# The gates of a two-layer encoder as one ScalarE Silu in place of Tanh, a scaled copy and a VectorE product

## The chip, the cores and the metric

The kernel runs on one core of one Trainium2 chip. The metric is the device time of one execution in microseconds (us), the median of the runs shown. A core has a matrix engine (TensorE; PE in the profile, PEld its weight loads), VectorE (DVE), ScalarE (ACT), GpSimd (POOL) and SyncE (SP); SP's and POOL's queues issue the DMA transfers here.

## What is computed

Two layers over 256 tokens of width 4096, in float32. Each layer normalises its input, projects it through one matrix of 4096 by 11264 into eight parts, runs 16 heads of attention (4 key and value heads) and 8 heads of a retention in both directions, gates both results by a silu of two of the projected parts, and projects the gated result back by a matrix of 4096 by 4096. Cut to what matters here:

```python
h = rmsnorm(x, norm_w[l])
proj = h @ w_in[l]
aq, ak, av, ag, rq, rk, rv, rg = jnp.split(proj, SPLIT_POINTS, axis=-1)
...
a_out = (jax.nn.silu(ag) * gqa_attention(aq, ak, av)).astype(x.dtype)
...
r_out = (jax.nn.silu(rg.astype(jnp.float32)) * r).astype(x.dtype)
x = x + jnp.concatenate([a_out, r_out], axis=-1) @ w_out[l]
```

The row's normalisation factor (`rstd`) is applied after the projection: the kernel multiplies the unnormalised input with the weights, and each consumer scales its part of the product by `rstd`, one number for each token.

## The kernel before

**Matrix products.** Each float32 operand is split into a high part, which TensorE takes in one pass, and a low part, the remainder; a product is three matmuls: high by high and low by high (line 1461), high by low (line 1471). The weights are the 512-wide side. They arrive from memory in raw tiles (`wraw`), are cast by ScalarE into the high part (`whi`), and VectorE subtracts to make the low part (`wlo`). Some row pairs use a scheme of seven products in place of eight, for which VectorE makes sums of the weights (`wsum`) first. High and low parts live in a ring of `RING` = 5 pages. A few pages are "far": GpSimd's queue makes their low part with an adding DMA (`fhi`, `flo`).

**Stages.** The work is 11 column blocks of the input projection and 4 of the output projection, for each of two layers. When a block is done, its result stands in two tiles `ca` and `cb` (tokens on the partitions, two row halves of 512 columns), and a task takes it: a gate is always `ca` of the blocks `ag` (four a layer, with the queries) and `rg` (four a layer, with the values). There are thus 16 gates in the program.

**Who follows a gate.** In `attention_group` the gated tile is transposed by VectorE (`turned`) and stored by four DMAs of POOL's queue to `g_dram`, to be fetched later and multiplied with the attention's result. In `retention_pair` the gate comes after the retention weights are there; then `values` makes the high and low part of the values (`vh` by ScalarE, `vl` by VectorE), then two times `retention_head` runs its products on TensorE and multiplies its result into the gate's tile.

**Order.** Every engine's order is written out in advance by a planner in the kernel's Python. `Clock` wraps VectorE and ScalarE: each recorded instruction adds an estimated cost to the engine's `until`, and `now.t` follows TensorE through 0.2268 us for each 512-wide matmul. Between matmuls `tick` asks `room` whether enough weight pages are ready ahead, and if so lets one of the waiting tasks do a step (up to a `yield`). After a step that ends in `yield "PE"` the task's matmuls are put `PE_REST` = 1.8 us behind its last planned instruction. The planner's costs:

```python
def vector_cost(name, n, kwargs):
    one = name in ("tensor_copy", "tensor_scalar", "tensor_scalar_mul", "tensor_scalar_add", "memset")
    return V_FIXED + n * (0.00052 if one else 0.00104)

def scalar_cost(name, n, kwargs):
    return S_FIXED + n * 0.00083 + (0.2 if kwargs.get("accum_out") is not None else 0.0)
```

with `V_FIXED` 0.07 and `S_FIXED` 0.16, and n the elements of a row. All VectorE and ScalarE instructions carry line 248, the line of the recorder, in the profile; they are told apart by their tiles. Working tiles come from 13 pages; a task starts only if the number of pages it pledges (`NEED`: 3 for `ag`, 4 for `rg`) is free.

**Other ScalarE functions.** Exp is used in the attention (`pr`, 64 instructions in 32 pairs) and for the retention's decay matrices (`D`, 8 instructions), and at the start; elsewhere there are copies, casts, squares and one Abs. Tanh occurs in the gates alone.

Of the kernel before, what the change touches and what calls it, by code (L numbers as in the profile page):

```python
# [13 lines left out]
AF = mybir.ActivationFunctionType  # L14
ALU = mybir.AluOpType
AX = mybir.AxisListType

P = 128
# [9 lines left out]
NB = 512  # L28
# [3 lines left out]
MT = SEQ // P  # L32
# [187 lines left out]
class Now:  # L220


    t = 0.0
# [39 lines left out]
def hybrid_encoder(  # L263
# [16 lines left out]
    ve, ac = Clock(nc.vector, vector_cost, now), Clock(nc.scalar, scalar_cost, now)  # L280
# [4 lines left out]
    sp = ctx.enter_context(tc.tile_pool(name="sp", bufs=1))  # L285
# [10 lines left out]
    def t(pool, shape, tag, bufs=None, dt=F32):  # L296
        kw = {} if bufs is None else {"bufs": bufs}
        return pool.tile(shape, dt, tag=tag, name=tag, **kw)
# [7 lines left out]
    def own(n):  # L306

        if current[0]:
            current[0].own += n

    def drop(n=1):

        held[0] -= n
        own(-n)

    def page(shape, name, dt=F32):

        held[0] += 1
        own(1)
        assert held[0] <= PAGES, name  # L320
        return sp.tile(shape, dt, tag="pg", name=name, bufs=PAGES)
# [69 lines left out]
    def rsqrt(dst, ss, n, count):  # L391

        ve.tensor_scalar(dst, ss, 1.0 / count, EPS, op0=ALU.mult, op1=ALU.add)
        nc.gpsimd.tensor_tensor(dst, dst, half[:, :n], op=ALU.pow)
# [617 lines left out]
    def gate(acc, L):  # L1012

        e = page([P, MT, NB], "tanh")
        for m in range(MT):
            h = L.hrstd[:, m : m + 1]
            ac.activation(e[:, m, :], acc[:, m, :], AF.Tanh, scale=h)  # L1020
            ac.activation(acc[:, m, :], acc[:, m, :], AF.Copy, scale=h)
        yield
        ve.scalar_tensor_tensor(acc, e, 1.0, acc, op0=ALU.add, op1=ALU.mult)
        drop()
        yield

    def attention_pair(g, h, kv, qT, rs, done):
# [69 lines left out]
    def attention_group(L, g, gacc, qacc):  # L1097
        def gates():
            yield from gate(gacc, L)
            room = page([P, KG * SEQ], "room")  # L1100
            turned(gacc, room)
            drop()
            yield 0.0
            store(room, g_dram[g % 2])

        yield from gates()
        while "aq" not in L.tables:
            yield
        rs = yield from rotary(qacc, L, "aq", q_dram[g % 2])
        yield STORE  # L1110
        L.rs[g] = rs
# [117 lines left out]
    def retention_pair(L, i, gacc, vacc):  # L1229
        while i not in L.weights:  # L1230
            yield
        wT = L.weights.pop(i)
        yield from gate(gacc, L)
        v = yield from values(vacc, L)
        yield
        for e in range(2):
            yield from retention_head(wT, v, gacc, e)
        users.discard(("h", L.index, i))
        own(2)
        drop(4)  # L1240
        pledge(2)
        room = page([P, KG * SEQ], "room")
        turned(gacc, room)
        if 4 + i < NCH - 2:
            drop()
            yield 0.0
            store(room, next_dram[4 + i])
            put(4 + i, None, 2 * L.index + 1)
        else:
            yield  # L1250
            mixT = gacc.rearrange("p m n -> p (m n)")
            yield from move(room, mixT)
            drop()
            put(4 + i, mixT, 2 * L.index + 1)
# [38 lines left out]
    def rstd_of(L, parts, n):  # L1293

        L.rstd = t(sp, [P, MT], "rstd", 2)
        L.hrstd = t(sp, [P, MT], "hrstd", 2)
        ve.tensor_reduce(L.rstd, parts, axis=AX.X, op=ALU.add)
        rsqrt(L.rstd, L.rstd, MT, D_MODEL)
        ve.tensor_scalar_mul(L.hrstd, L.rstd, 0.5)

    def in_task(L, kind, i, c):
        while L.rstd is None:
# [221 lines left out]
    def out_task(l, n, res):  # L1524
# [19 lines left out]
        if n == N_OUT - 1:  # L1544
            rstd_of(layers[l + 1], sums[:, :, :N_OUT], N_OUT)
# [111 lines left out]
    def first_sums():  # L1657
        load_small()
        part = t(sp, [P, MT, N_OUT], "sums", 2)
        loaded = []  # L1660
        for n in range(N_OUT + 2):
            if n < N_OUT:
                loaded.append(page([P, MT, NB], "x"))
                nc.sync.dma_start(loaded[-1], rows(x[:, columns(n)]))
            yield LANDING / 2
            if n >= 2:
                v = loaded.pop(0)
                for m in range(MT):
                    ac.activation(v[:, m, :], v[:, m, :], AF.Square, accum_out=part[:, m, n - 2 : n - 1])
                drop()  # L1670
        rstd_of(layers[0], part[:, :, :N_OUT], N_OUT)
        whole = page([P, 2 * SEQ], "dist")
        nc.sync.dma_start(whole, consts[:, C_D:C_END])
        yield LANDING / 2
        ac.copy(dist, whole)
        drop()
        log_sigmoid()
        yield
# [154 lines left out]
```

## Time and profile before

| what | value |
|---|---|
| median of 3 runs | 2624.57 us (2623.66 to 2625.17) |
| the profiled execution's own time | 2624.09 us |
| its span, first to last instruction | 2622.3 us |
| granted TensorE clock, mean | 0.998 |
| TensorE busy | 2604.2 us, 99% |
| VectorE busy | 2231.7 us, 85% |
| ScalarE busy | 1684.6 us, 64% |

The span is what the profile shows; the execution's own time is 1.8 us longer. The rows that the prediction quotes come from the profile's page, from groups of instructions (count, busy time, mean duration, idle time just before them and who ended it), from waits (who waited for whom: total, times, longest), from tables of stretches of the span, and from the timeline (start, duration, engine, line, operation, tiles, and in brackets the idle time before it).

### The profile page before, as it was taken

The numbers are of one execution on the slowest core, as the hardware profiler recorded it, in microseconds if no ns is written. First come the engines' busy times: TensorE is split into PE (matmuls) and PEld (weight loads), VectorE is DVE, ScalarE is ACT, GpSimd is POOL, SyncE is SP. The second block draws the span as 40 slices with busy tenths as digits, with TensorE's granted clock in tenths as the row PEclk, the third lists the DMA queues.
The fourth block names the chain that finished last, engine by engine and source line by source line (L and its number), as shares of the span: only waits on it lengthen the run. The fifth ranks groups of instructions, "written<-read, shape, count | busy, mean of one in ns | idle before, by whom it ended". The sixth has DMA issues, their size and how long they took to land.

```text
span 2622.3 us, 33965 instructions
## 1 busy us (share of the span) xinstructions
PE 2604.2 (99%) x11650; PEld 2151.5 (82%) x11650; DVE 2231.7 (85%) x2666; ACT 1684.6 (64%) x2411; POOL 274.6 (10%) x413
## 2 busy tenths in 40 slices
PE   9999999999999999999999999999999999999998
PEld 7888888888888888888888888888888888878886
DVE  8798988898878889777998889898997798897768
ACT  7776667656555778556785666676565566775545
POOL 0010221120001000111101101211100010000000
PEclk9999999999999999999999999999999999999999
DMA  7888887877667766777767777778766666656775
GB/s 287 291 263 261 266 266 240 295 241 235 211 217 235 232 227 214 259 261 255 276 219 230 257 237 265 255 239 276 249 225 209 217 227 217 227 201 220 240 235 188
DMA packets 187151, 633.58 MB, mean 242 GB/s; under 512 B 22624, under 2 KB 29280, under 8 KB 186976
## 3 DMA queue, kind: packets, MB, share of 16 engines
q1 hardware_dynamic: 147760, 521.27, 56.6%
q0 software_dynamic: 39216, 110.12, 15.9%
q8 instruction: 91, 1.49, 0.2%
q14 instruction: 84, 0.69, 0.1%
HBM read 587.27 MB, written 44.04 MB: 241 GB/s over the span
## 4 chain that ended last, share of the span: by engine, by line
PE 94%; DVE 3%; issue 1%; ACT 1%; DMA 1%; SPq 0%; DVEq 0%; POOLq 0%; POOL 0%; ACTq 0%
PE M L1461 60%; PE M L1471 30%; DVE wlo L248 1%; PE M L945 1%; PE M L944 1%; PE M L943 1%; DMA wraw<-in_w_in 1%; DVE wsum L248 1%; PE M L1455 0%; ACT whi L248 0%; ACT ca L248 0%; DMA flo<-in_w_in 0%; DVE ca L248 0%; DVE x7l L248 0%; DVE ls L248 0%
## 5 line engine op out<-in xcount | busy, mean ns | idle before, releaser
L248 ACT CAST whi<-wraw 128x1024 fp32r<-128x1024 f32 (+1 forms) x912 | 878.5, 978 | 529.8 <-PE M L1461 346.2
L248 DVE TENSOR_TENSOR wlo<-wraw,whi 128x1024 fp32r<-128x1024 f32 (+1 forms) x912 | 1007.5, 1127 | 156.3 <-ACT whi L248 147.6
L1461 PE MATMUL M<-whi,x8h 128*128 128x512 f32 x2042 | 795.7, 390 | 0.2 <-DVE cb L248 0.2
L1461 PE MATMUL M<-whi,x8l 128*128 128x512 f32 x2042 | 795.2, 389 | 0.0
L1471 PE MATMUL M<-wlo,x8h 128*128 128x512 f32 x2042 | 586.3, 389 | 0.0
L1461 PE MATMUL M<-whi,x7h 128*128 128x512 f32 x1442 | 561.2, 389 | 1.0 <-ACT whi L248 1.0
L1461 PE MATMUL M<-whi,x7l 128*128 128x512 f32 x1442 | 561.0, 389 | 0.0
L248 ACT CAST whi<-wsum 128x1024 fp32r<-128x1024 f32 x300 | 315.9, 1053 | 212.4 <-PE M L1461 105.2
L1461 PEld LDWEIGHTS M<-whi,x8h 128*128 128x128 f32 x2042 | 383.4, 188 | 80.8 <-DVE cb L248 1.3
L1461 PEld LDWEIGHTS M<-whi,x8l 128*128 128x128 f32 x2042 | 383.4, 188 | 79.0 <-DVE x7l L248 0.2
L1471 PEld LDWEIGHTS M<-wlo,x8h 128*128 128x128 f32 x2042 | 382.1, 188 | 78.8
L1471 PE MATMUL M<-wlo,x7h 128*128 128x512 f32 x1442 | 442.1, 390 | 2.7 <-DVE wlo L248 2.4
L248 DVE TENSOR_TENSOR wlo<-wsum,whi 128x1024 fp32r<-128x1024 f32 x300 | 365.9, 1220 | 42.6 <-ACT whi L248 42.4
L1471 PEld LDWEIGHTS M<-wlo,x7h 128*128 128x128 f32 x1442 | 269.5, 188 | 63.3 <-DVE wlo L248 8.2
L1461 PEld LDWEIGHTS M<-whi,x7h 128*128 128x128 f32 x1442 | 270.7, 188 | 57.8 <-ACT whi L248 1.4
L1461 PEld LDWEIGHTS M<-whi,x7l 128*128 128x128 f32 x1442 | 270.7, 188 | 56.3
L248 DVE TENSOR_TENSOR wsum<-wraw 128x1024 f32<-128x1024 f32 x150 | 182.5, 1216 | 29.9 <-DMA wraw<-in_w_out 14.0
L506 POOL DMA_DIRECT2D flo<-in_w_in x32 | 29.2, 912 | 819.5 <-ACT flo L248 814.4
L248 DVE TENSOR_TENSOR wsum<-wsum,wraw 128x512 f32<-128x512 f32 x150 | 103.8, 692 | 5.2
L248 DVE TENSOR_TENSOR wsum<-wraw,wsum 128x512 f32<-128x512 f32 x150 | 102.4, 683 | 0.1
L248 DVE TENSOR_TENSOR cb<-cb,M 128x512 f32<-128x512 f32 x90 | 60.8, 679 | 23.8 <-PE M L1471 23.8
L248 ACT ACTIVATE pr<-M,st,rs 128x256 f32<-128x256 f32 x64 | 35.5, 559 | 48.5 <-DVE st L248 48.5
(232 smaller groups left out, 1961.3 us busy)
## 6 DMA issues: line engine op xcount, KB each, us to landing
wraw<-in_w_in SPq DMA_DIRECT2D x700, 512.0 KB, 4.5
wraw<-in_w_out SPq DMA_DIRECT2D x256, 512.0 KB, 4.4
flo<-in_w_in POOLq DMA_DIRECT2D x32, 512.0 KB, 7.4
full<-next_dram POOLq DMA_DIRECT2D x18, 512.0 KB, 8.4
kv<-kv_dram POOLq DMA_DIRECT2D x16, 512.0 KB, 7.4
p_dram<-room POOLq DMA_DIRECT2D x64, 128.0 KB, 2.9
pT<-p_dram POOLq DMA_DIRECT2D x16, 512.0 KB, 9.3
flo<-in_w_out POOLq DMA_DIRECT2D x11, 512.0 KB, 7.6
```

Of the source, the lines that this page charges most:

```text
L248: return call(out, *args, **kwargs)
L506: nc.gpsimd.dma_start(g.lo[h], g.src[0][:, h, :], accum_op=ALU.add)
L943: nc.tensor.matmul(out, a[0], b[0], start=start, stop=False)
L944: nc.tensor.matmul(out, a[0], b[1], start=False, stop=False)
L945: nc.tensor.matmul(out, a[1], b[0], start=False, stop=stop)
L1461: nc.tensor.matmul(acc[name], a[i], g.hi[h], start=m == first[name] and not i, stop=False)
L1471: nc.tensor.matmul(acc[name], a, g.lo[h], start=False, stop=m == final[name])
```

## The change

`gate` is Silu with the row's `rstd` as its scale, in place, one instruction for each row half. The Tanh into a page of its own, the copy scaled by half of `rstd`, VectorE's (tanh + 1) times the copy, the page, one `yield`, and the tile `hrstd` go.

```diff
@@ gate
-        e = page([P, MT, NB], "tanh")
         for m in range(MT):
-            h = L.hrstd[:, m : m + 1]
-            ac.activation(e[:, m, :], acc[:, m, :], AF.Tanh, scale=h)
-            ac.activation(acc[:, m, :], acc[:, m, :], AF.Copy, scale=h)
-        yield
-        ve.scalar_tensor_tensor(acc, e, 1.0, acc, op0=ALU.add, op1=ALU.mult)
-        drop()
+            ac.activation(acc[:, m, :], acc[:, m, :], AF.Silu, scale=L.rstd[:, m : m + 1])
         yield
@@ rstd_of
         L.rstd = t(sp, [P, MT], "rstd", 2)
-        L.hrstd = t(sp, [P, MT], "hrstd", 2)
         ve.tensor_reduce(L.rstd, parts, axis=AX.X, op=ALU.add)
         rsqrt(L.rstd, L.rstd, MT, D_MODEL)
-        ve.tensor_scalar_mul(L.hrstd, L.rstd, 0.5)
```

## The prediction

> **What bounds the kernel now.** I read the page's busy line first, then a table of stretches of the span, then TensorE's own waits. In the table the columns are the stretch, its length, and for PE, PEld, DVE, ACT and POOL the busy time with the instruction count in brackets; then the granted clock, the DMA share and GB/s.
>
> ```profile
> PE 2604.2 (99%) x11650; PEld 2151.5 (82%) x11650; DVE 2231.7 (85%) x2666; ACT 1684.6 (64%) x2411; POOL 274.6 (10%) x413
> ...
> 0.00:25.00 25.00, 23.05 (x71) 12.59 (x72) 13.02 (x21) 16.49 (x30) 0.20 (x4) 1.00 0.92 348
> 25.00:590.00 565.00, 564.77 (x2530) 467.60 (x2529) 499.86 (x616) 382.50 (x589) 85.08 (x130) 1.00 0.81 264
> 590.00:600.00 10.00, 9.03 (x40) 6.95 (x39) 8.16 (x10) 6.53 (x10) 0.00 (x0) 1.00 0.63 230
> 600.00:1020.00 420.00, 420.00 (x1920) 350.22 (x1919) 357.64 (x438) 278.22 (x382) 33.75 (x48) 1.00 0.68 223
> 1020.00:1040.00 20.00, 19.67 (x85) 15.63 (x85) 19.90 (x25) 17.42 (x25) 0.90 (x1) 1.00 0.74 236
> 1275.00:1320.00 45.00, 44.58 (x194) 35.59 (x193) 44.39 (x63) 34.07 (x53) 3.58 (x4) 1.00 0.76 239
> 2325.00:2345.00 20.00, 18.42 (x79) 14.34 (x78) 18.95 (x24) 15.01 (x23) 0.00 (x0) 1.00 0.48 168
> 2345.00:2609.00 264.00, 263.68 (x1162) 217.52 (x1161) 206.76 (x225) 141.40 (x175) 9.51 (x11) 1.00 0.67 220
> 2609.00:2622.30 13.30, 1.03 (x5) 0.53 (x3) 4.42 (x10) 2.84 (x6) 0.56 (x1) 0.69 0.84 311
> ```
>
> TensorE is the bound, and nearly without holes. Of the 18.1 us in which it is idle (2622.3 less 2604.2), 1.95 lie in the first 25 us and 12.27 in the tail after the last products. Between, 3.85 us are left: 0.23 before 590, 0.97 around 595, 0.33 around 1030, 0.42 around 1300, 1.58 around 2335 and 0.32 after it. Where it runs, 420 us hold 1920 matmuls, 0.219 us each, at a granted clock of 1.00. Who ends its idle time:
>
> ```profile
> PE M L1471 <- DVE wlo L248: 2.4, 5, 1.3
> PEld M L1471 <- DVE wlo L248: 8.2, 15, 1.7
> ```
>
> The holes are low halves of the weights that VectorE brings late (8.2 us in 15 waits on the weight-load side, parts of which the pipelined matmuls cover). So a change on ScalarE or VectorE moves the time only by making such waits, or by taking some of these few microseconds away. How much the gates' engines have to spare where the gates run is the next table: 12 us around four of the gates, and the sum over such stretches around all 16.
>
> ```profile
> 710.00:722.00 12.00, 12.00 (x56) 10.01 (x55) 10.37 (x12) 8.88 (x11) 0.00 (x0) 1.00 0.37 132
> 882.00:894.00 12.00, 12.00 (x58) 10.05 (x57) 11.04 (x13) 8.87 (x11) 0.00 (x0) 1.00 0.39 137
> 972.00:984.00 12.00, 12.00 (x54) 9.94 (x53) 11.58 (x23) 11.94 (x23) 0.00 (x0) 1.00 0.53 182
> 2270.00:2282.00 12.00, 12.00 (x55) 9.91 (x54) 11.58 (x22) 11.94 (x23) 0.00 (x0) 1.00 0.54 181
> sum 192.00, PE 192.00 PEld 159.20 DVE 177.93 ACT 168.40 POOL 32.76; mean PE 12.00 PEld 9.95 DVE 11.12 ACT 10.52 POOL 2.05
> ```
>
> TensorE is busy 192.00 of 192.00 us: no gate costs it anything today. ScalarE and VectorE are crowded there (168.4 and 177.9), most of all at the last gate of each layer, 972 and 2270.
>
> **What goes.** The groups of the gate (busy us in all, mean ns of one, idle before), and the one table load of the program:
>
> ```profile
> L248 ACT ACTIVATE ca<-ca,hrstd 128x512 f32<-128x512 f32 x32 | 23.2, 726 | 1.0
> L248 ACT ACTIVATE tanh<-ca,hrstd 128x512 f32<-128x512 f32 x32 | 22.9, 715 | 0.2 <-DVE ca L248 0.2
> L248 ACT ACT_TABLE_LOAD x1 | 1.3, 1283 | 0.7 <-PEq L1822 0.7
> ...
> L248 DVE SCALAR_TENSOR_TENSOR ca<-tanh,ca 128x1024 f32<-128x1024 f32 x16 | 19.6, 1225 | 8.8 <-ACT ca L248 8.5
> L248 DVE TENSOR_SCALAR hrstd<-rstd 128x2 f32<-128x2 f32 x2 | 0.3, 170 | 1.7 <-POOL rstd L394 1.7
> ```
>
> Sixteen gates, two row halves each. The 32 scaled copies go: 23.2 us of ScalarE. The 16 products go: 19.6 us of VectorE, with 8.8 us of its waiting for ScalarE just before them. The two `hrstd` multiplications go, 0.3 us and 1.7 us of waiting. The page `tanh` goes, but each gate's task pledges 3 or 4 pages whether it holds them or not, so no other task starts earlier for it. All this is beside a TensorE that is busy 192.00 of 192.00 us: worth nothing by itself.
>
> **What comes.** 32 Silu in the place of 32 Tanh: same shape, same per-row scale operand, so I take the Tanh's 715 ns, and the difference is nothing. What the trace doesn't show is whether Silu lives in the table that is loaded once at the start and serves Exp and Tanh alike. If it does, no load is added. If not, each gate that follows an Exp loads a table and each Exp that follows a gate loads the other: at most 16 and 16, 32 times 1.283 = 41 us of ScalarE. I take the loads as coming, as the dearer end. The Trainium skill, ScalarE: Activation LUTs, section What ACT_TABLE_LOAD costs, gives 2.66 us for a switch, the 1.28 us load and a drain of 1.38 us; by that it would be an estimated 85 us of ScalarE, and the load row above bears out the 1.28, while no row shows the drain, as nothing runs ahead of that load.
>
> Where the loads fall decides. First the way back to Exp:
>
> ```profile
> 0.74 1.28 ACT L248 ACT_TABLE_LOAD   x1 [0.74 <-PEq L1822]
> 2.03 0.22 ACT L248 ACTIVATE lg<-half 128x16 f32<-128x16 f32 x1
> ...
> 0.81 0.07 DVE L248 MEMSET half<- 128x16 f32 x1 [0.81 <-PEq L1822]
> ...
> ACT pr L248 <- DVE st L248: 49.5, 19, 4.4
> ACT D L248 <- DVE D L248: 16.3, 8, 2.7
> ```
>
> The load began at 0.74, before the operand of its Exp was begun (0.81): it doesn't sit behind the Exp's wait. And an Exp that follows a gate usually finds ScalarE idle: all 8 Exps of the decay matrices wait, 2.0 us on average, and those of the attention 19 times, 2.6 us on average. A load of 1.28 us goes into that idle time. So the way back costs nothing in most places; where it isn't hidden, it delays casts by 1.3 us, and for these there is the lead below.
>
> Then the gate itself, here the one at 712:
>
> ```profile
> 710.43 2.00 ACT L248 CAST whi<-wraw 128x1024 fp32r<-128x1024 f32 x2 [4.38 <-PE M L1461]
> 712.33 0.72 ACT L248 ACTIVATE tanh<-ca,hrstd 128x512 f32<-128x512 f32 x1
> 713.72 0.71 ACT L248 ACTIVATE tanh<-ca,hrstd 128x512 f32<-128x512 f32 x1
> 715.09 1.04 ACT L248 CAST whi<-wraw 128x1024 fp32r<-128x1024 f32 x1
> 716.04 1.33 ACT L248 ACTIVATE vh<-cb,rstd 128x512 fp32r<-128x512 f32 x2
> 718.63 1.41 DVE L248 SCALAR_TENSOR_TENSOR vl<-cb,rstd,vh 128x512 fp32r<-128x512 f32 x2
> 721.67 0.28 PE L944 MATMUL M<-vl,wTh 128*128 128x256 f32 x1
> ...
> ACT whi L248 <- PE M L1461: 451.3, 436, 4.4
> ```
>
> The gate now holds ScalarE from 712.33 to 715.09, 2.76 us. After the change it is 1.28 for the load and two Silu at the step from one Tanh to the next halved, (713.72 − 712.33) / 2 = 0.70 each: 2.68 us. ScalarE is done 0.1 us sooner, and VectorE has 1.23 us less to do. With a drain as long as the load (an estimate from the load's row, 1.28) it is 3.96, 1.2 us later. Either is below the lead of the casts: they go round a ring of five pages, 436 of them wait for TensorE to free a place, 451 us in all, and the pair just before this gate waited 4.38 us for that. A cast that waits so has four filled pages ahead of it; four pages of a seven-product pair hold 7 products of 3 matmuls, 7 · 3 · 0.219 = 4.6 us, and those of plain pairs 4 · 4 · 3 · 0.219 = 10.5 us. Nothing becomes late by 1.2 us. Next is the product that the gate's task issues: TensorE reads `vl` at 721.67, `vl` ends at 720.04, 1.63 us earlier, and began 1.26 us after `vh` ended (717.37). So there are 2.9 us between `vh` and the matmul.
>
> Last, the planner. It writes the order of the engines from its own costs, here (0.16 + 512 · 0.00083) = 0.585 us for each gate instruction on ScalarE and 1.13 us for VectorE's. It will see 1.17 us in place of 2.34, and nothing on VectorE, and know of no load; so the steps after a gate move up by 1 to 2 us, in the order of ScalarE, VectorE and TensorE alike. Where they stand then I can't read from this trace. Bounds: below, the late low halves at 1030 and 2335, in stages that the crowded gates 972 and 2270 run into, go away: −(0.33 + 1.58) = −1.9 us. Above, all holes between 25 and 2609 double: +3.85. I take 0, since at all 16 gates the nearest rows show TensorE without any idle time.
>
> **Sum.** ScalarE −23.2 + 41 (none of it ahead of TensorE), VectorE −19.6 (none ahead of TensorE), planner 0: the profiled execution stays at 2624.1 (span 2622.3 and 1.8 around it). The median of the runs shown, 2624.57, is 0.5 above that, so 2624.6. 0.2% is 5.2 us, about what a measurement of this kernel can tell from no change.
>
> **Rivals.**
>
> *Every switch reaches TensorE.* The Trainium skill, ScalarE: Activation LUTs, section Table sets: the hidden batching unit, says to batch calls by table set and not by function, and this change does the opposite, putting Silu between Exps. The mechanism here: the gates' loads, unknown to the planner, use up the lead. That decides if casts at the gates have less than 1.28 us of it. Price: 16 loads of 1.28 = 20.5, so 2645. For it: the ScalarE rows at 972 and 2270, 11.94 of 12. Against: the 4.38 us wait just ahead of the load, and the copies' 1.4 us given back in the same place.
>
> *The values come late.* The planner's view of a gate is off by 2.76 − 2.34 = 0.42 us today; it would be off by 2.68 − 1.17 = 1.51, or 2.79 with the drain, 1.1 to 2.4 us more. `retention_pair` goes from the gate straight to `values` and to products whose place in TensorE's order is planned from there. With VectorE's product gone, `vl` can stand right behind `vh`, and the 1.26 us between them is no longer there; then 2.4 less the remaining 1.63 is a stall of 0.8 us at each of 8 retention gates: +6.2, so 2631. It decides from a lateness of 1.63 us; with the bare load, 1.1, there is none.
>
> *VectorE's relief fills the holes.* The holes are late low halves, and VectorE gets 19.6 us. All of them gone is −3.85: 2620.7. Against: of the holes only those at 1030 and 2335 come within 65 us behind a gate. It isn't even 0.2%.
>
> *No loads at all*, since Silu is in the table of Exp: ScalarE falls by 23 us, the time is the same 2624.6.
>
> **How the numbers follow.** Forecast, with or without loads, within a few microseconds: 0.69. Holes filled: 0.10, half of it counted as over 0.2% for what pipelined matmuls hide of the 8.2 us. Late values or another planned step that comes late, 5 to 8 us: 0.14. Every switch: 0.07. Faster 0.05, same 0.74, slower 0.21. The range goes from the filled holes, 2620.7, to the late values with a little of the doubled holes at the stage ends, 2632; every switch and half of the filled holes are left out.
>
> **What would show it.** Table loads: some 30 of 1.28 us, those before Exp in idle time ended by VectorE; ScalarE about 18 us up, VectorE 20 us down; the windows around the gates still with TensorE at 12.00. Wrong it is if waits of TensorE for `whi`, `wlo` or `vl` appear within 15 us behind a gate, or if the stages at 595, 1030, 1300 and 2335 show several times their idle time.

## The result and the profile after

The change makes the kernel slower by a little: 2630.09 us (2628.11 to 2631.64, 13 runs) against 2623.76 (2623.25 to 2625.6, 13 runs), a ratio of 1.0023 with a 95% interval of 1.0015 to 1.0032. Forecast was 2624.6, with a range from 2620.7 to 2632. The profiled execution took 2629.94 us, its span is 2628.2.

First the page's busy line and the stretches that answer to those of before (columns as there; the time has moved by 1 to 6 us, so the last two are cut a little later), with the stretch from 2190 to 2300 added:

```profile
PE 2606.6 (99%) x11650; PEld 2151.0 (82%) x11650; DVE 2214.9 (84%) x2648; ACT 1697.1 (65%) x2408; POOL 273.8 (10%) x413
...
25.00:590.00 565.00, 563.28 (x2520) 465.66 (x2519) 494.75 (x610) 386.80 (x589) 84.98 (x130) 1.00 0.79 263
590.00:600.00 10.00, 9.41 (x41) 7.32 (x40) 7.25 (x8) 4.78 (x6) 0.00 (x0) 1.00 0.68 250
600.00:1020.00 420.00, 418.78 (x1912) 348.46 (x1911) 355.16 (x438) 283.48 (x390) 34.39 (x48) 1.00 0.68 224
1020.00:1040.00 20.00, 20.00 (x90) 16.56 (x89) 19.34 (x23) 14.96 (x18) 0.89 (x1) 1.00 0.67 207
2190.00:2300.00 110.00, 107.01 (x491) 87.19 (x490) 97.44 (x144) 83.02 (x143) 6.23 (x9) 1.00 0.59 202
2325.00:2345.00 20.00, 20.00 (x90) 16.55 (x89) 18.99 (x21) 12.61 (x14) 0.00 (x0) 1.00 0.55 183
```

VectorE has 16.8 us less to do, as taken out, and ScalarE 12.5 us more. The holes at 1030 and 2335 are gone. New ones stand in 600 to 1020 (1.22 us) and in 2190 to 2300 (2.99 us), where TensorE had none before, and in 25 to 590 (1.72 us, 0.23 before). Who ends them, for TensorE's matmuls and then, for 2190 to 2300 alone, its weight loads:

```profile
PE M L1453 <- DVE cb L248: 3.6, 4, 1.3
PE M L1453 <- ACT whi L248: 2.1, 3, 1.2
PE M L1463 <- DVE wlo L248: 0.8, 4, 0.3
...
PEld M L1463 <- DVE wlo L248: 2.9, 5, 0.7
PEld M L1453 <- ACT whi L248: 2.1, 2, 1.6
PEld M L1453 <- DVE cb L248: 1.4, 1, 1.4
```

Late low halves were known from before. Late `cb`, the adding up of a finished block, is nearly new (one wait of 0.2 us before). Late high halves have grown; before, there was one, the hole around 595, in a row that the prediction doesn't show:

```profile
PE M L1461 <- ACT whi L248: 1.0, 1, 1.0
```

Short holes don't show in the stretches, as the matmuls overlap; laid matmul by matmul against the profile of before, TensorE ends 5.5 us later. The delay grows by 5.3 us between 2190 and 2300 and by 1.9 us between 890 and 1000; 0.9 us is given back at 1030 and 2.2 us at 2335, where the old holes are gone. 1.4 us arise at 95, ahead of the first gate, where both programs are the same (1.3 us of the waits for `cb` above are there). The second profile of the change (below) has 0.5 us there, and a run without loads 0.3, so the rest belongs to that execution and not to the change.

What the table loads do is seen in ScalarE's groups:

```profile
L248 ACT ACT_TABLE_LOAD x30 | 38.5, 1283 | 27.5 <-DVE st L248 22.4 <-DMA pT<-p_dram 4.0 <-PEq L1814 0.7
L248 ACT ACTIVATE ca<-ca,rstd 128x512 f32<-128x512 f32 x44 | 29.4, 716 | 0.8 <-DVE ca L248 0.7
```

29 loads came, 15 ahead of a gate and 14 on the way back, each 1283 ns. The 32 Silu are among the 44 of the second row (12 scaled copies of keys have the same tiles); the mean is 716 ns, that of the Tanh. The number to see is the 27.5 us of idle time just before the loads, 22.4 of them ended by `st`: those loads began when the wait was over. With the 4.0 us ended by `pT`, they are 8 loads, each ahead of an Exp of the attention.

### The profile page after: what moved, and what is told of

Same layout as the page of the kernel before. It is cut to its first block, busy times and chain, and to the rows that moved or that the text cites. A ratio compares the mean times of both kernels' runs of the same rounds, so it can differ in the third digit from the quotient of the medians.

```text
span 2628.2 us, 33961 instructions
## 1 busy us (share of the span) xinstructions
PE 2606.6 (99%) x11650; PEld 2151.0 (82%) x11650; DVE 2214.9 (84%) x2648; ACT 1697.1 (65%) x2408; POOL 273.8 (10%) x413
## 4 chain that ended last, share of the span: by engine, by line
PE 87%; DVE 6%; DMA 3%; issue 2%; ACT 2%; SPq 0%; POOL 0%; DVEq 0%; POOLq 0%; ACTq 0%
PE M L1453 56%; PE M L1463 28%; DVE wlo L248 3%; DMA wraw<-in_w_in 3%; PE M L945 1%; PE M L944 1%; PE M L943 1%; ACT whi L248 1%; DVE wsum L248 1%; DVE x7l L248 0%; ACT ca L248 0%; DVE xf L248 0%; DVE cb L248 0%; DVE x8l L248 0%; DMA full<-in_xT 0%
## 5 line engine op out<-in xcount | busy, mean ns | idle before, releaser
L248 ACT CAST fhi<-wraw 128x1024 fp32r<-128x1024 f32 (+1 forms) x44 | 45.9, 1043 | 28.1 <-PE M L1453 28.1
```

The costliest lines, as they stand in the source:

```text
L248: return call(out, *args, **kwargs)
```

## The experiments

Two theories were set against each other: LOADS, that the added loads reach TensorE, and ORDER, that the planner, which sees a shorter gate, writes an order that collides somewhere. The first four runs separate them by two means: Tanh in the place of Silu keeps the order and has no loads, and charging the planner for what is no longer there keeps the order of before. The diffs of the second and third run are cut and stand against the kernel before, the others against the change.

**The order of the change, without loads.**

```diff
-            ac.activation(acc[:, m, :], acc[:, m, :], AF.Silu, scale=L.rstd[:, m : m + 1])
+            ac.activation(acc[:, m, :], acc[:, m, :], AF.Tanh, scale=L.rstd[:, m : m + 1])
```

> The changed kernel with Tanh written where it has Silu: the same planner costs, so the same order on every engine, the same durations, but no table load beyond the first. The gates hold tanh(x) and not silu(x) here. Theory LOADS (the 6.3 us come from the 29 added table loads of 1.283 us reaching TensorE through late casts and subtractions): 2624 us, within 1.5 of the kernel before. Theory ORDER (the planner sees a gate 1.17 us shorter on ScalarE and gone from VectorE, and the order that it writes collides at a few places, loads or not): 2629 to 2631, with the same holes of TensorE at about 973, 2210 to 2235 and 2275.

2626.28 us (11 runs), 1.0004 of before (0.9995 to 1.0012). Between the two theories: LOADS isn't the whole, nor is ORDER.

**The order of before, with Silu and its loads.**

```diff
-        e = page([P, MT, NB], "tanh")
+        page([P, MT, NB], "tanh")
...
+            ac.activation(acc[:, m, :], acc[:, m, :], AF.Silu, scale=L.rstd[:, m : m + 1])
+            ac.until += scalar_cost("activation", NB, {})
         yield
-        ve.scalar_tensor_tensor(acc, e, 1.0, acc, op0=ALU.add, op1=ALU.mult)
+        ve.until = max(ve.until, now.t) + vector_cost("scalar_tensor_tensor", MT * NB, {})
```

> Silu in place as in the change, but the planner is charged for the instructions that are no longer there (a second ScalarE instruction for each half, VectorE's product, the page and the yield), so that the order of all engines is that of the kernel before. 29 table loads remain. Theory LOADS: 2628 to 2630. Theory ORDER: 2623 to 2624.5, at the kernel before or a little under it, since VectorE has 19.6 us and ScalarE 23.2 us less to do in the same order.

2626.76 us, 1.0007 (0.9998 to 1.0016). TensorE's instructions stand in the order of before, all 11,650. Again in the middle.

**The kernel before, with loads added.**

```diff
+        nc.scalar.activation(dummy, half, AF.Silu)
         for m in range(MT):
             h = L.hrstd[:, m : m + 1]
```

> The kernel before with one tiny Silu (128 x 16, its result unused, about 0.2 us) ahead of each gate, unknown to the planner: the order and all work of before, plus the 29 table loads and 16 tiny instructions, with nothing given back. This is the loads' price alone, and 1.5 us more on ScalarE at each gate than the change has. Theory LOADS: 2630 or more. Theory ORDER: 2624 to 2626.

2633.61 us (5 runs), 1.0035 (1.0021 to 1.0049). Without the relief, the loads and the 16 tiny Silus together cost 8.7 us against 2624.94 for the kernel before in that session.

**The planner told of the loads.**

```diff
+            if name == "activation" and args[1] in (AF.Exp, AF.Silu):
+                if args[1] != self.table:
+                    self.until = max(self.until, self._now.t) + LOAD
+                self.table = args[1]
```

> The change, with the planner charged 1.3 us on ScalarE whenever the function goes from Exp to Silu or back, so that its view of ScalarE is right again. Theory LOADS (late because unplanned): 2624 to 2626, the planner leaves room for them. Theory ORDER: yet another order with other collisions, anything from 2623 to 2632; no reason for it to be better than the change.

2629.95 us, 1.0019 (1.0010 to 1.0028). LOADS missed here: a right view of ScalarE doesn't help. The planner writes another order again, with holes at other places (about 265, 595 and 1565).

The second group adds the missing corner of the square, Tanh in the order of before:

> Tanh alone in place (the gates hold tanh(x), not silu(x)), with the planner charged as for the kernel before: the order of before, the relief of 23.2 us on ScalarE and 19.6 us on VectorE, and no added load. With Silu in the same order the run was 2626.8, with late matmuls around 305, 1615 and 2585. If the loads make these, they are gone here: 2623 to 2625, and what VectorE's relief is worth by itself is the distance to the kernel before, at most 2 us (the holes at 1030 and 2335). If they come from the taken-out work itself (casts and weight transfers that start at other times), they stay: 2626 to 2628.

2623.09 us, 0.9995 (0.9986 to 1.0003). Now the parts add up, in medians: from 2623.1, the loads alone give 2626.8 (+3.7), the order alone 2626.3 (+3.2), both 2630.3 (+7.2, the change measured once more beside this run, below). The relief by itself is 2625.1 − 2623.1 = 2.0 us, though its interval still holds no change. These are differences of medians, in part from two sessions (the kernel before took 2624.94 and 2625.11 in them), and each run's interval reaches about 2.2 us either way. So a difference of 6 us is clear; one of 2 to 4 us is not by itself, and leans on where the traces show it.

**Where the loads bite.** Between these two runs of one order, TensorE's delay grows in steps of 0.5 to 1.3 us around 305, 595, 1615, 2335 and 2585. The stretch before the one at 1615, of the run with Silu (timeline of ScalarE, then of SP's queue, then a stretch):

```profile
1566.02 1.28 ACT L248 ACT_TABLE_LOAD   x1
1567.32 1.34 ACT L248 ACTIVATE ca<-ca,rstd 128x512 f32<-128x512 f32 x2
1569.89 1.28 ACT L248 ACT_TABLE_LOAD   x1 [1.24 <-DVE st L248]
1571.19 0.56 ACT L248 ACTIVATE pr<-M,st,rs 128x256 f32<-128x256 f32 x1
...
1592.64 10.80 SPq L448 DMA_DIRECT2D wraw<-in_w_in  x6
...
1606.09 1.57 ACT L248 CAST whi<-wraw 128x1024 fp32r<-128x1024 f32 x2 [4.16 <-DMA wraw<-in_w_in]
...
1605.00:1615.00 10.00, 9.32 (x41) 7.11 (x40) 5.50 (x6) 4.84 (x6) 0.00 (x0) 1.00 0.90 355
```

and of the run with Tanh:

```profile
1588.99 15.77 SPq L448 DMA_DIRECT2D wraw<-in_w_in  x8
...
1601.50 1.57 ACT L248 CAST whi<-wraw 128x1024 fp32r<-128x1024 f32 x2 [2.22 <-DMA wraw<-in_w_in]
...
1605.00:1615.00 10.00, 10.00 (x46) 8.27 (x45) 7.72 (x9) 5.37 (x7) 0.00 (x0) 1.00 0.80 305
```

Here a gate stands between two Exps of one attention pair, so ScalarE loads twice within 4 us, and the second load begins only after the idle time. ScalarE is behind by the two loads, frees the raw tiles later, and SP's next burst of weight transfers goes out at 1592.64 and not 1588.99 (1.2 of these 3.65 us are TensorE's own delay in that profile up to there). The transfers then run at 355 GB/s, the cast at 1606.09 waits 4.16 us for them, and TensorE loses 0.68 us in ten. So the lag isn't given back in the 35 us between, though ScalarE has idle time there: by 1587 ScalarE's casts are only TensorE's own 1.2 us behind, while the burst still goes out 3.65 us late. The lag has been handed on to the transfers. That the freed tiles are what holds the burst is read from the kernel's order of calls; it wasn't tried alone.

**Loads moved into the idle time.** In front of each attention Exp that follows a gate, a tiny Exp of a constant:

```diff
+            if table[0] != "exp":
+                nc.scalar.activation(dummy, half, AF.Exp)
+            table[0] = "exp"
             for m in range(MT):
                 i = 2 * e + m
```

> Silu in the order of before, as in the second run, with a tiny Exp of a constant tile (16 wide) in front of each attention Exp that follows a gate. It has nothing to wait for, so the load back to Exp's table can run while ScalarE waits for VectorE's maxima; in the changed kernel 8 of the 14 loads back sit behind that wait. Theory LOADS BEHIND THE WAIT: the lag of 1.3 us that ScalarE takes along from 271 and 1572 shrinks, TensorE's loss around 305 and 1615 (0.9 and 1.3 us in the second run) falls to under 0.4 each, total 2624.5 to 2625.5. Rival, LOADS AT THE GATE (the load ahead of Silu alone makes the lag): no change against 2626.8, within 0.7.

2622.47 us, 0.9993 (0.9984 to 1.0001), 4.3 us under the same kernel without the tiny Exps and at the value of the run without loads. In the total LOADS BEHIND THE WAIT holds, more strongly than expected. Of the two places that it named, the loss at 1615 is gone; at 305 this profile still loses 1.1 us against the run with Tanh. It is the profile of one of the two slowest executions (2625.17), and the repeat of this kernel (below) loses next to nothing there (0.15), so what happens at 305 isn't set by the loads behind the wait alone. The way back in the change, and then in this run:

```profile
249.74 1.06 ACT L248 CAST whi<-wraw 128x1024 fp32r<-128x1024 f32 x1 [0.72 <-PE M L1453]
254.78 1.28 ACT L248 ACT_TABLE_LOAD   x1 [3.99 <-DVE st L248]
256.08 0.56 ACT L248 ACTIVATE pr<-M,st,rs 128x256 f32<-128x256 f32 x1
...
249.09 1.28 ACT L1047 ACT_TABLE_LOAD   x1
250.38 0.22 ACT L1047 ACTIVATE dummy<-half 128x16 f32<-128x16 f32 x1
253.07 0.57 ACT L248 ACTIVATE pr<-M,st,rs 128x256 f32<-128x256 f32 x1 [2.47 <-DVE st L248]
```

In the change ScalarE idles 3.99 us and loads then. In this run the load runs at once, in the first part of the same idle time.

The same in the order of the change:

> The change itself with the same 8 tiny Exps. LOADS BEHIND THE WAIT: 1 to 2 us under the change in the same session, through 305 and 1615; the losses at 973 and 2270, which the run without loads has too, stay. LOADS AT THE GATE: equal to the change.

2628.59 us, 1.0015 (1.0006 to 1.0023).

> The change once more, beside the others on one chip. 2629 to 2631. In its first profile TensorE lost 1.4 us around 95, ahead of the first gate, where the program doesn't differ from before; if that is chance and not the change, it is absent or of another size here.

2630.33 us (10 runs), 1.0023 (1.0014 to 1.0033), and 0.5 us at 95 in place of 1.4. So the tiny Exps bring 1.7 us here (the two intervals overlap); between the two profiles the losses at 305 and 1615 shrink by 0.4 and 1.0 us. Another 1.5 us between them, at 2275, isn't the tiny Exps' doing: there the second profile of the change has a granted clock of 0.85 over 2270 to 2280, the first one and the run with the tiny Exps 1.00.

6.1 us against the same kernel in the order of before are left with the order of the change. They aren't all the order's own: the run with Tanh in this order, which has no loads, is only 3.2 us above its pair. Laid against that run, the run with the tiny Exps loses 0.5 us around 915 and 1.3 us around 2220, as both profiles of the change do; in the order of before nothing is lost there. Ahead of both places stands a load that the tiny Exps don't move, the one for the Exp of the last block's decay matrices (here the later one, and the stretch behind it):

```profile
2206.33 1.28 ACT L248 ACT_TABLE_LOAD   x1
...
2210.00:2230.00 20.00, 19.56 (x83) 15.16 (x83) 17.56 (x23) 17.80 (x30) 0.00 (x0) 1.00 0.57 186
```

In the run with Tanh this Exp has no idle time ahead of it and TensorE is busy for all 20.00 us. So the load had nothing to hide in, and ScalarE is 1.3 us later behind it. In medians the loads still cost 2628.6 − 2626.3 = 2.3 us in this order. No run moved this load alone.

**One gate or many.** In the profile of before the second retention head of the third block runs its products at 955, one stretch after the first; in the change at 898, a few us after it. `room` let it in because the gate was over sooner in the planner's view. That tests ORDER at one place; the tiny Exps are in both of the next runs.

```diff
-        yield from gate(gacc, L)
+        yield from gate(gacc, L, i != 2)   # charged as before, but for the third block
```

> Silu with the early tiny Exps. The planner is charged as for the kernel before at 15 or rather 14 of the 16 gates, and sees the shorter gate, as in the change, only at the third retention block of each layer (the gates at about 884 and 2182). There the second retention head comes into the same stretch as the first instead of the next, and with it the last block's weights move towards the end of the block, where TensorE lost its time at 973 and 2270. Theory ONE GATE: nearly the whole loss by the order is here, 2625.5 to 2628.5 against 2622.5 with all gates charged. Rival, MANY SMALL: the loss is spread over the gates, 2623 to 2624.

2628.67 us, 1.0016 (1.0007 to 1.0025): with 2 of 16 gates seen as shorter, the whole 6 us.

> The complement: the planner sees the shorter gate at the other 14 gates and is charged as before only at the third retention block of each layer. ONE GATE: 2622 to 2624.5. MANY SMALL: 2626 to 2628.6, near the change with the early Exps (2628.6).

2624.55 us, 1.0001 (0.9992 to 1.0010): with the other 14 seen as shorter, 4 us less, at the upper edge of what ONE GATE expects. It is 1.9 us above the run with all charged in the same session (below); the intervals overlap. Stretches of the two, first e9, then e10:

```profile
900.00:1000.00 100.00, 98.56 (x449) 81.14 (x448) 87.55 (x128) 78.04 (x126) 7.28 (x10) 1.00 0.70 219
2190.00:2300.00 110.00, 107.12 (x484) 87.06 (x483) 95.58 (x142) 81.73 (x140) 6.21 (x9) 0.98 0.61 201
2300.00:2350.00 50.00, 50.00 (x222) 41.42 (x221) 44.27 (x50) 36.51 (x53) 0.00 (x0) 1.00 0.55 187
...
900.00:1000.00 100.00, 100.00 (x465) 83.61 (x464) 83.23 (x115) 76.47 (x122) 6.99 (x10) 1.00 0.70 221
2190.00:2300.00 110.00, 110.00 (x514) 92.13 (x513) 95.12 (x136) 82.52 (x136) 7.14 (x9) 1.00 0.62 205
2300.00:2350.00 50.00, 49.42 (x216) 40.08 (x215) 48.41 (x61) 39.11 (x62) 0.00 (x0) 1.00 0.59 194
1000.00:1045.00 45.00, 42.16 (x181) 33.33 (x180) 43.40 (x57) 37.34 (x59) 0.92 (x1) 1.00 0.60 195
```

The holes of 1.4 and 2.9 us come and go with that one gate of each layer. The last row limits this: in e10 a hole of 2.8 us stands at 1000 to 1045 in the first layer, where the run with all gates charged has 0.3. So the other 14 gates move the order too, and what they cost there is as much as the hole that is gone; the clear gain is in the second layer. (e9's profile, with 2631.22 the slowest of its 11 executions, also has a granted clock of 0.83 over 2270 to 2280, as the second profile of the change has 0.85.) What most of the larger hole consists of, from VectorE's timeline in the change, with the first matmul that waits:

```profile
2271.79 0.28 DVE L248 TENSOR_TENSOR xf<-xf,full 128x128 f32<-128x128 f32 x1
2272.10 0.29 DVE L248 SCALAR_TENSOR_TENSOR xf<-xf,full 128x128 f32<-128x128 f32 x1
2272.31 0.28 DVE L248 TENSOR_TENSOR xf<-full 128x128 f32<-128x128 f32 x1
2272.51 0.28 DVE L248 TENSOR_TENSOR xf<-full,xf 128x128 f32<-128x128 f32 x1
2272.72 0.69 DVE L248 SCALAR_TENSOR_TENSOR D<-M,D 128x512 f32<-128x512 f32 x1
2273.32 0.41 DVE L248 TENSOR_TENSOR x7l<-full,x7h 128x256 fp32r<-128x256 f32 x1
2273.65 0.83 DVE L248 TENSOR_TENSOR x7l<-xf,x7h 128x640 fp32r<-128x640 f32 x1
2274.60 1.23 DVE L248 TENSOR_TENSOR wlo<-wraw,whi 128x1024 fp32r<-128x1024 f32 x1
2275.74 0.68 DVE L248 TENSOR_TENSOR cb<-cb,M 128x512 f32<-128x512 f32 x1
2276.34 1.22 DVE L248 TENSOR_TENSOR wTl<-D,wTh 128x1024 fp32r<-128x1024 f32 x1
2277.47 0.68 DVE L248 TENSOR_TENSOR cb<-cb,M 128x512 f32<-128x512 f32 x1
...
2276.57 0.47 PE L1453 MATMUL M<-whi,x8h 128*128 128x512 f32 x1 [1.17 <-ACT whi L248]
```

With the head finished a stretch earlier, its tile is turned earlier, and the next stage's operands (`xf`, `x7l`) are split inside the last block, right at its end, where the score product (`D`) of the last retention weights has slid to as well. That queue stands before the two additions into `cb`, and TensorE, which uses the banks that they read again, waits for the second one; the matmul at 2276.57 waited 1.17 us before that for a cast, which ScalarE brought late in the same crowd. In the order of before the score product runs at 2260 and the five splits of the stage are spread from 2273 to 2311, without a hole of TensorE there; the hole of 1.58 at 2335 comes after them, and the change has none at 2335. That the one stands for the other is read from the order of the two, not tried. The rest of the 2.99 us are short waits for low and high halves from 2214 to 2252.

**The best version again, and with the attention's gates uncharged.**

> The version of the sixth run once more (Silu, order of before, early tiny Exps), on the same chip as the two before it: 2622 to 2623.5, 0.0005 to 0.001 under the kernel before.

2622.67 us, 0.9992 (0.9983 to 1.0000).

> Silu with the early tiny Exps; the planner sees the shorter gate only at the 8 attention gates. TensorE's order is that of the kernel before, instruction by instruction; VectorE's differs in some places. If the order costs only where the retention's gates move it: 2622 to 2623.5, as the sixth run. If any step that moves costs: 2624 or more.

2622.55 us, 0.9990 (0.9981 to 0.9998): steps that move at the attention's gates cost nothing that shows. These three runs, 2622.5 to 2622.7 against 2624.9 to 2625.1, lie below both kernels; against the kernel before, only the last one's interval is clear of no change.

## Why the prediction was right and wrong

The measured time lies in the range, but the sum's 0 was wrong by 6 us, and the likeliest case, within a few microseconds, wasn't what happened. That the range holds it is luck: its upper end came from values that arrive late at TensorE, and no such wait showed.

- *The terms of the work* held: Silu as long as Tanh (716 and 715 ns), 29 loads of 1283 ns where at most 32 were counted, VectorE 17 us down; ScalarE went up by 12.5 us, where about 18 were forecast. The relief is worth about 2.0 us, and the bound of the prediction for it was 1.9, in part by chance: the bound was the holes at 1030 and 2335, and between the profiles of before and of the run with Tanh in its order 0.5 and 0.8 us are won there, but 1.1 us at 595. The prediction read all holes as late low halves of VectorE; the one at 595 waited for a high half of ScalarE. The drain of 1.28 us that was kept as an upper end isn't seen here: the load at 714.25 follows a cast that ends at 714.24, and the Silu starts 0.02 us after the load's end.

```profile
712.23 2.01 ACT L248 CAST whi<-wraw 128x1024 fp32r<-128x1024 f32 x2 [4.39 <-PE M L1453]
714.25 1.28 ACT L248 ACT_TABLE_LOAD   x1
715.55 1.34 ACT L248 ACTIVATE ca<-ca,rstd 128x512 f32<-128x512 f32 x2
716.79 1.32 ACT L248 ACTIVATE vh<-cb,rstd 128x512 fp32r<-128x512 f32 x2
```

  The gate holds ScalarE for 2.54 us (714.25 to 716.79), 2.68 were forecast, 2.76 it was. By the Trainium skill, ScalarE: Activation LUTs, section What ACT_TABLE_LOAD costs, a switch would take 2.66 us; this trace shows its load and not its drain.

- *"So the way back costs nothing in most places"* was the first step that failed. It rested on one row, the load at the start, which ran ahead of its Exp's wait. The attention's Exps wait for two engines, VectorE and TensorE; in the trace of the change the wait for VectorE (`st`) stands at the load itself and the wait for TensorE at the Exp behind it, so the load starts after the idle time. The Exps of the decay matrices have one wait, and there the load does run ahead (the one at 869.86 began at once, and its Exp 1.30 us after its end). The attention's idle time that was counted as cover thus wasn't any, and with the cover gone the price was not the 1.3 us on casts that have lead, but 4.3 us of the total in the order of before and 1.7 in that of the change. In the order of the change the step failed a second time, with loads of the decay matrices that found no idle time any more.

- *"Nothing becomes late by 1.2 us"* was true within 12 us of a gate: around 712 TensorE is busy without a hole. It failed 35 us later, around 1615, where the lead is short for another reason, the transfers. The lead was read at the gates only, and the lag was taken to end with ScalarE's next idle time.

- *"Planner 0"* was the second step that failed: it is 3.2 us without loads and 6.1 with the attention's loads back hidden, of which traces put about 1.8 on loads that the new order leaves uncovered. The bound of 3.85, all holes doubled, was near the first and below the second, and the rival "another planned step that comes late, 5 to 8 us", had 0.14 with the late values. The place given was wrong: no TensorE wait for `vl` showed; it was a head of the third block that slipped into an earlier stretch. The signs that the prediction named, waits within 15 us behind a gate or more idle time in the stages known for it, were too narrow: the new holes stand 25 to 90 us behind the gate that causes them, and the known ones at 1030 and 2335 are gone, as in its best case.

- *Every switch reaches TensorE*, priced at 20.5 us: it didn't. 29 loads cost 3.7 to 4 us. Once 8 of them are moved ahead of the wait, they cost about nothing in the order of before (2622.5 with 29, 2623.1 with none) and 2.3 us in that of the change. So the price is that of the few loads that stand behind a wait, or where there is no idle time. The Trainium skill, ScalarE: Activation LUTs, section Table sets: the hidden batching unit, has the rule to batch calls by table set; in the order of before, the run with the early tiny Exps alternates the sets with 29 loads and shows no loss by it.

## What to carry to other kernels

In these runs a table load cost little where ScalarE was idle, and its full length plus what hung on it where it came behind a wait or where no idle time was left; a tiny call of the next function, with nothing to wait for, moved it out of the wait. Where a planner writes the order, taking out work changes two things, the work and the order; charge the planner for the old work once, to see each by itself before judging the edit. Lead must be read where it is shortest downstream, not where the delay arises.

## What the runs showed of the hardware

A load for an Exp with two waits started only when one of them was over (3.99 us idle, then 1.28 us of load), one for an Exp with a single wait at once (at 869.86, 1.30 us ahead of need). A switch of tables took 1.28 us and 0.03 of gaps, with no drain to be seen. In two of the five profiles that have the large hole at about 2275 (the second of the change and e9), TensorE's granted clock was 0.85 and 0.83 over 2270 to 2280; in the others (the change's first, the run with Tanh in its order, the one with tiny Exps) it was 1.00. What decides that, the runs don't show. And a lag of ScalarE of some 2 us lived on through the weight transfers for 35 us, although ScalarE was busy only 4.63 and 4.01 us in two stretches of ten between (Silu in the order of before):

```profile
1585.00:1595.00 10.00, 10.00 (x46) 8.29 (x45) 9.93 (x13) 4.63 (x5) 0.93 (x2) 1.00 0.41 147
1595.00:1605.00 10.00, 10.00 (x46) 8.28 (x45) 9.92 (x11) 4.01 (x4) 4.02 (x8) 1.00 1.00 338
```
